# Later landings in the plan, one more known reader, and order lists searched anew, in a hybrid decoder block

## The chip, the cores and the metric

The kernel runs on one core of a Trainium2 chip. The metric is device time in microseconds from launch to end, the median of three runs. PE is the matrix engine (TensorE), DVE the vector engine, ACT the scalar engine, POOL the engine that issues the adding transfers (GpSimd), SP the engine that issues the loads (SyncE).

## What is computed

One decoder block over 256 positions of width 2048: a half-step SwiGLU feed-forward, a token mixer (a recurrent branch and a short gated convolution that share one input projection), and a second half-step feed-forward, with RMS norms between. The change touches the two feed-forwards alone:

```
def swiglu_ffn(x, w_gate, w_up, w_down):
    return (jax.nn.silu(x @ w_gate) * (x @ w_up)) @ w_down

x = x + 0.5 * swiglu_ffn(rms_norm(x, ffn1_norm), ffn1_w_gate, ffn1_w_up, ffn1_w_down)
...                                                   # the mixer
x = x + 0.5 * swiglu_ffn(rms_norm(x, ffn2_norm), ffn2_w_gate, ffn2_w_up, ffn2_w_down)
```

`w_gate` and `w_up` are 2048 by 5632, `w_down` 5632 by 2048, all float32.

## The kernel before

**Arithmetic.** A float32 operand is split into a high part (`hi`, a cast by ACT) and a low part (`lo`, the difference, by DVE). A product of two is three matmul passes: high by high and low by high (the "high products", `Unit.over`), and high by the weight's low part (the "low products", `Unit.under`). Each matmul takes a 128 by 128 block of the activations as the stationary operand and streams 512 columns of weights.

**Strips.** The 5632 columns of gate and up are eleven blocks of 512. One goes through plain products at the opening; the other ten go in pairs. A pair of blocks is a *strip*, and `sevens` (from L690 on) computes it by a two-by-two block scheme with seven products instead of eight: p0 to p6 for most of the depth, and plain products x01, x00, x11, x10 for the rows left over. Strip names give the matrix (g, u, d), the feed-forward (1 or 2) and a number: g1_4 is a gate strip of feed-forward 1, u1_4 its up strip, d1_2 a stage of down strips. The weights of p4, p5, p6 and p3 are sums of loaded blocks (w11, w12, w21, w22). DVE adds them in place in w11 (for p4, then for p5); some are added by a transfer that POOL issues (`by_transfer`, L719).

**Banks.** Sums gather in PSUM banks a, c, d and e. p0 goes to a, and ACT copies it to d ("seed"). p4 goes to bank c, and ACT takes a copy of it ("s5") before x01 adds to c; x01 starts bank e afresh. In a *joint* strip p4 goes to bank e, ACT copies e to c, and x01 adds onto both, so that one DVE addition of s5 at the end falls away. p5 and p6 leave the copies u2 and u3.

**Hidden units.** A gated result (`u_g`, `z`) of 128 by 512 is turned by eight transposes on PE for two positions' blocks (tile `ph`), and ACT and DVE then write its high and low parts into `h`, the stationary operand of the down strips. The items T, U are these turns in an order list. Tiles `split_..._x..` (the x weights of gate and up, under pair names "xa" and "xb") and `h` share one pool, `bigs`, of nine places: a new `h` takes a place that such a `split` tile may still hold, and its writers then wait until the last matmul has read it.

**What sets the order.** A table gives PE's order for each strip: `FINE_ORDERS` for gate and up (L31), `DOWN_ORDERS` for down (L65). The first letter says whether p3's sum is made by DVE (+, J) or by a transfer (-, j), J and j mean joint; 5 or 6 in gate and up says how the spare row is treated. For ACT, DVE, SP and POOL the class `Plan` (from L160) makes the order when the kernel is built: each step has an engine, a length, needs and a due time; `Plan.run` (L249) simulates the engines and takes the most pressing ready step. These orders are then fixed in the program. On the chip each engine runs its queue strictly in order, with semaphores for the needs; a step that waits holds all behind it. A load is planned with

```
step = self.add("SP", 0.45, fn, tail=1.5 + 0.71 * rows)
step.room, step.share = room, ("load", 1.35, 0.71 * rows, 0.6)
```

where 1.35 is the start and 0.6 the tail behind a queue that loads share with the adding transfers. The places `short`, one alone in gate and up, hold the x weights: the next x load is issued when DVE has read the one before.

`turn_item` (L1452) plans a turn and its two copies; `turn_cells` (L1529) calls it for T and U. The last turn of an up stage is handed over, with its PE step's end as the earliest time, to the next `down_stage` (L1621), which plans its copies. Neither knew of the `bigs` place that an `h` takes.

## Time and profile before

| | |
|---|---|
| median of three runs | 1711.32 us (1710.82 to 1712.18) |
| profiled execution, its own time | 1713.96 us |
| its span, first to last instruction | 1712.2 us |
| granted clock of PE, mean | 0.996 |
| matmuls on PE | 7706 |

| stage | span from the start, us | PE busy, us | granted clock |
|---|---|---|---|
| gate and up 1, first pairs (g1_1 to u1_2) | 200.4 to 363.5 | 162.65 of 163.10 | 1.00 |
| down d1_2 | 363.5 to 453.4 | 85.02 of 89.90 | 0.98 |
| g1_3 to u1_4 | 453.4 to 619.6 | 164.29 of 166.20 | 0.99 |
| down d1_4 | 619.6 to 704.0 | 84.40 of 84.40 | 1.00 |
| mixer | 704.0 to 1015.0 | 310.34 of 311.00 | 1.00 |
| g2_1 to u2_2 | 1205.7 to 1369.8 | 162.44 of 164.10 | 1.00 |
| down d2_2 | 1369.8 to 1453.5 | 83.08 of 83.70 | 1.00 |
| g2_3 to u2_4 | 1453.5 to 1619.9 | 164.39 of 166.40 | 0.99 |

How rows are read: in the order in time, a row is start, duration, engine, line, instruction, operands, shape, count, and in square brackets the engine's idle time before it with what ended it. Buffer numbers are left out, so `hi_g_p<-raw_g_w` may be any p's high part of a gate strip. L102 is the helper that records every instruction. In a row of stretches, PE, PEld, DVE, ACT and POOL busy time stand with their counts, then the granted clock, the share of the DMA engines and GB/s. The matmul's own duration includes its pipeline; rows of a run of matmuls are best compared from start to start.

### The profile page before, as it was taken

How to read it: one execution, taken by the hardware profiler on the slowest of the kernel's cores; microseconds unless marked ns; L12 is line 12 of the kernel's file. 1: busy time of each engine (PE TensorE's matmuls, PEld its weight loads, DVE VectorE, ACT ScalarE, POOL GpSimd, SP SyncE). 2: the span in 40 equal slices, each digit the busy share in tenths (PEclk: the TensorE clock that was granted, in tenths of full speed). 3: DMA queues.
4: the chain of work that ended last, by engine and by line, in shares of the span. 5: the costliest groups of instructions: out<-in, count | busy, mean ns of one | idle time of the engine just before them, and what ended most of it. 6: DMA issues, size and time to landing. Idle time of an engine off the chain costs nothing.

```text
span 1712.2 us, 20073 instructions
## 1 busy us (share of the span) xinstructions
PE 1688.8 (99%) x7706; PEld 1399.1 (82%) x7706; DVE 1557.0 (91%) x1281; ACT 1127.1 (66%) x1305; POOL 85.5 (5%) x107
## 2 busy tenths in 40 slices
PE   9999999989999999999999999999999999999997
PEld 7888888878887888888888888888887888887886
DVE  7989999989989998899997978998999899989996
ACT  6766576746675767688776665756666666756665
POOL 0200000000000000000000000000000000000000
PEclk9999999999999999999999999999999999999999
DMA  8786988867988868577856685967978777988784
GB/s 320 238 236 202 277 251 256 268 194 222 283 275 230 268 203 267 189 226 243 260 198 204 214 270 172 288 234 221 307 240 257 238 240 248 274 257 238 251 256 143
DMA packets 187744, 413.48 MB, mean 241 GB/s; under 512 B 8324, under 2 KB 11264, under 8 KB 184320
## 3 DMA queue, kind: packets, MB, share of 16 engines
q1 hardware_dynamic: 174912, 340.81, 56.2%
q0 software_dynamic: 12560, 70.33, 21.5%
q8 instruction: 60, 0.98, 0.2%
q10 hardware_dynamic: 176, 1.06, 0.2%
q14 instruction: 36, 0.29, 0.1%
HBM read 339.82 MB, written 2.10 MB: 200 GB/s over the span
## 4 chain that ended last, share of the span: by engine, by line
PE 89%; DVE 5%; DMA 2%; issue 2%; ACT 2%; DVEq 0%; SPq 0%; ACTq 0%
PE ps_g_a L102 10%; PE ps_d_a L102 9%; PE ps_u_a L102 8%; PE ps_d_c L102 6%; PE ps_g_c L102 6%; PE ps_u_c L102 5%; PE ps_d_d L102 4%; PE ps_u_d L102 3%; PE ps_d L102 3%; PE ps_d_e L102 3%; PE ps_g_d L102 3%; PE ps_in_b L102 3%; PE ps_in_x L102 3%; PE ps_u_e L102 3%; PE ps_o L102 3%; PE ps_u L102 2%
## 5 line engine op out<-in xcount | busy, mean ns | idle before, releaser
L102 DVE TENSOR_TENSOR lo_g_p<-raw_g_w,hi_g_p 128x3072 fp32r<-128x3072 f32 (+3 forms) x90 | 234.8, 2625 | 29.3 <-ACT hi_g_p L102 13.0
L102 ACT CAST hi_g_p<-raw_g_w 128x1536 fp32r<-128x1536 f32 (+1 forms) x140 | 200.1, 1466 | 79.0 <-DVE raw_g_w L102 25.0
L102 DVE TENSOR_TENSOR lo_u_p<-raw_u_w,hi_u_p 128x3072 fp32r<-128x3072 f32 (+3 forms) x90 | 221.2, 2464 | 21.6 <-ACT hi_u_p L102 21.5
L102 ACT CAST hi_u_p<-raw_u_w 128x1536 fp32r<-128x1536 f32 (+1 forms) x140 | 188.7, 1386 | 73.2 <-DVE raw_u_w L102 34.5
L102 ACT CAST hi_d_p<-raw_d_w 128x1024 fp32r<-128x1024 f32 x140 | 141.6, 1048 | 96.0 <-DVE raw_d_w L102 59.8
L102 DVE TENSOR_TENSOR lo_d_p<-raw_d_w,hi_d_p 128x2048 fp32r<-128x2048 f32 (+1 forms) x90 | 161.3, 1811 | 7.7 <-ACT hi_d_p L102 7.1
L102 DVE TENSOR_TENSOR raw_u_w<-raw_u_w,raw_u_w 128x1024 f32<-128x1024 f32 (+2 forms) x49 | 84.5, 1734 | 3.0 <-DMA raw_u_w<-in_ffn_w_up_dram 1.9
L102 ACT CAST hi_d_x<-raw_d_x 128x1024 fp32r<-128x1024 f32 x72 | 73.2, 1046 | 17.9 <-DMA raw_d_x<-in_ffn_w_down_dram 7.4
L102 DVE TENSOR_TENSOR lo_d_x<-raw_d_x,hi_d_x 128x2048 fp32r<-128x2048 f32 x36 | 82.0, 2285 | 2.6 <-ACT hi_d_x L102 2.1
L102 ACT CAST split_u_x<-raw_u_x 128x1024 fp32r<-128x1024 f32 x40 | 42.0, 1051 | 55.8 <-DMA raw_u_x<-in_ffn_w_up_dram 55.7
L102 PE MATMUL ps_u_a<-hi_u_p,xT_n 128*128 128x512 f32 x280 | 73.5, 390 | 0.0
L102 DVE TENSOR_TENSOR raw_g_w<-raw_g_w,raw_g_w 128x1536 f32<-128x1536 f32 (+2 forms) x41 | 70.8, 1752 | 0.3
L102 PE MATMUL ps_g_a<-hi_g_p,xT_n 128*128 128x512 f32 x280 | 70.3, 389 | 0.0
L102 ACT CAST split_g_x<-raw_g_x 128x1024 fp32r<-128x1024 f32 x40 | 41.9, 1047 | 40.9 <-DMA raw_g_x<-in_ffn_w_gate_dram 40.6
L102 PEld LDWEIGHTS ps_g_a<-hi_g_p,xT_n 128*128 128x128 f32 x280 | 52.6, 188 | 10.9
L102 PEld LDWEIGHTS ps_u_a<-hi_u_p,xT_n 128*128 128x128 f32 x280 | 52.3, 188 | 10.7
L717 POOL DMA_DIRECT2D raw_g_w<-raw_g_w x38 | 33.0, 867 | 553.7 <-DVE raw_g_w L102 333.9
L102 DVE TENSOR_TENSOR raw_d_w<-raw_d_w,raw_d_w 128x1024 f32<-128x1024 f32 (+1 forms) x43 | 54.6, 1293 | 0.3
L102 DVE TENSOR_TENSOR split_u_x<-raw_u_x,split_u_x 128x1024 fp32r<-128x1024 f32 x40 | 48.8, 1219 | 5.5 <-ACT split_u_x L102 5.5
L102 DVE TENSOR_TENSOR split_g_x<-raw_g_x,split_g_x 128x1024 fp32r<-128x1024 f32 x40 | 48.8, 1219 | 2.4 <-ACT split_g_x L102 2.4
L102 PE MATMUL ps_d<-hi_d,h 128*128 128x512 f32 x192 | 45.8, 391 | 0.0
L102 PEld LDWEIGHTS ps_d<-hi_d,h 128*128 128x128 f32 x192 | 35.8, 188 | 7.3
(579 smaller groups left out, 4178.3 us busy)
## 6 DMA issues: line engine op xcount, KB each, us to landing
raw_g_w<-in_ffn_w_gate_dram SPq DMA_DIRECT2D x40, 1024.0 KB, 6.7
raw_u_w<-in_ffn_w_up_dram SPq DMA_DIRECT2D x40, 1024.0 KB, 7.3
raw_d_w<-in_ffn_w_down_dram SPq DMA_DIRECT2D x40, 1024.0 KB, 6.8
raw_d_x<-in_ffn_w_down_dram SPq DMA_DIRECT2D x36, 1024.0 KB, 6.6
raw_g_w<-raw_g_w POOLq DMA_DIRECT2D x37, 768.0 KB, 8.2
raw_g_w<-in_ffn_w_gate_dram SPq DMA_DIRECT2D x40, 512.0 KB, 7.5
raw_g_x<-in_ffn_w_gate_dram SPq DMA_DIRECT2D x40, 512.0 KB, 5.6
raw_u_w<-in_ffn_w_up_dram SPq DMA_DIRECT2D x40, 512.0 KB, 7.7
```

The costliest lines, as they stand in the source:

```text
L102: ins = getattr(self.engine, name)(*args, **kwargs)
L717: nc.gpsimd.dma_start(raw[key]()[:, h, :], raw[other]()[:, h, :], accum_op=ALU.add)
```

## The change

Three things. A load and an adding transfer are planned to land 0.5 us later. The copies of a turned unit get one more need: the last low product of the `split` tile given up (`after`), and those handed over to the down stage start no earlier than the last such product of the stage (`used`). And the order lists are other ones: 14 of 20 for gate and up, 9 of 10 for down. Seven strips become joint and one ceases to be.

```
 def load(self, rows, fn, room):
-    step = self.add("SP", 0.45, fn, tail=1.5 + 0.71 * rows)
-    step.room, step.share = room, ("load", 1.35, 0.71 * rows, 0.6)
+    step = self.add("SP", 0.45, fn, tail=2.0 + 0.71 * rows)
+    step.room, step.share = room, ("load", 1.35, 0.71 * rows, 1.1)
...
-    z = plan.add("POOL", ..., tail=6.7 + 1.36 * more)
-    z.share = "sum", 1.8, 5.43 + 1.36 * more, 0.6
+    z = plan.add("POOL", ..., tail=7.2 + 1.36 * more)
+    z.share = "sum", 1.8, 5.43 + 1.36 * more, 1.1
...
-    return turned_parts(plan, high, low, a, at=since)
+    return turned_parts(plan, high, low, a, after, at=since)
...
-    turn_before = lambda z=before: turn_cells(plan, [z[1, 0], z[0, 0]], turned)
+    def turn_before(z=before, given_up=short_turn[1]):
+        turn_cells(plan, [z[1, 0], z[0, 0]], turned, after=plan.left[given_up].low)
...
-    return plan, tails, [(*z[:3], z[3].end - end) for z in later]
+    used = max(plan.left[p].low.end for p in ("xa", "xb") if p in plan.left)
+    return plan, tails, [(*z[:3], max(z[3].end, used) - end) for z in later]
...
 FINE_ORDERS, (2, 1), last list (u2_2); DOWN_ORDERS, (1, 2), first list
-["J5", "p0", "U", "p4", "p5", "x01", "p2", "x11", "p6", "x00", "p1", "T", "x10", "p3"]
+["J5", "p0", "p4", "x01", "p5", "p2", "x11", "p6", "x00", "U", "p1", "T", "p3", "x10"]
-["-", "p0", "T", "p4", "x01", "x11", "p5", "p1", "p6", "x00", "p3", "p2", "x10"]
+["j", "p0", "p4", "T", "x01", "x11", "p5", "p1", "p6", "x00", "p3", "p2", "x10"]
```

The program keeps every matmul, every transfer and every ACT instruction in number; DVE has 1275 instructions instead of 1281. Where they stand differs. Three places:

ACT at the entry of the down strip d1_2_0; `h1_6` is the unit turned last in the up strip. Before:

```order
L102 CAST split_u1_2_x10_2777<-raw_u1_2_x10_2754 128x1024
L102 CAST hi_d1_2_0_p0_2883<-raw_d1_2_0_w11_2875 128x1024
L102 CAST h1_6_2889<-ph1_6_1_2795 128x4x128
L102 CAST h1_6_2889<-ph1_6_0_2800 128x4x128
L102 CAST hi_d1_2_0_p0_2883<-raw_d1_2_0_w11_2875 128x1024
L102 CAST hi_d1_2_0_x01_2900<-raw_d1_2_0_x01_2879 128x1024
L102 CAST hi_d1_2_0_p4_2903<-raw_d1_2_0_w11_2875 128x1024
L102 CAST hs1_2_4_0_2906<-hv1_4_1_2891 128x512
L102 CAST hi_d1_2_0_x01_2900<-raw_d1_2_0_x01_2879 128x1024
L102 CAST hi_d1_2_0_p4_2903<-raw_d1_2_0_w11_2875 128x1024
```

With the change:

```order
L102 CAST split_u1_2_x10_2771<-raw_u1_2_x10_2737 128x1024
L102 CAST hi_d1_2_0_p0_2877<-raw_d1_2_0_w11_2873 128x1024 x2
L102 CAST hi_d1_2_0_x01_2893<-raw_d1_2_0_x01_2879 128x1024
L102 CAST hs1_2_4_0_2897<-hv1_4_1_2888 128x512
L102 CAST hi_d1_2_0_p4_2899<-raw_d1_2_0_w11_2873 128x1024
L102 CAST h1_6_2902<-ph1_6_1_2826 128x4x128
L102 CAST h1_6_2902<-ph1_6_0_2831 128x4x128
L102 CAST hi_d1_2_0_p4_2899<-raw_d1_2_0_w11_2873 128x1024
L102 CAST hi_d1_2_0_x01_2893<-raw_d1_2_0_x01_2879 128x1024
L102 CAST hi_d1_2_0_x11_2931<-raw_d1_2_0_x11_2881 128x1024 x2
```

The two copies of `h1_6` moved from between the two halves of p0 to behind p0, half of x01, `hs` and half of p4.

ACT at the start of the second gate strip g1_4, from the copy of p0 (seed) on. Before:

```order
L102 COPY ps_g1_4_d_4122<-ps_g1_4_a_4088 128x512
L102 CAST hi_g1_4_p5_4132<-raw_g1_4_w11_3904 128x1536
L102 ACTIVATE s5_g1_4_4148<-ps_g1_4_c_4115 128x512
L102 CAST hi_g1_4_p1_4150<-raw_g1_4_w21_4032 128x1536
L102 CAST hi_g1_4_p5_4132<-raw_g1_4_w11_3904 128x1536
L102 CAST hi_g1_4_p1_4150<-raw_g1_4_w21_4032 128x1536
```

With the change:

```order
L102 COPY ps_g1_4_d_4118<-ps_g1_4_a_4085 128x512
L102 CAST hi_g1_4_p1_4130<-raw_g1_4_w21_4031 128x1536
L102 ACTIVATE s5_g1_4_4144<-ps_g1_4_c_4111 128x512
L102 CAST hi_g1_4_p5_4146<-raw_g1_4_w11_3931 128x1536 x2
L102 CAST hi_g1_4_p1_4130<-raw_g1_4_w21_4031 128x1536
```

The copy s5 stood behind p5's first half; now p1's first half stands there and p5 comes after s5. In g2_2 and g2_4 the rows around s5 are the same in both programs; on DVE one of the two z's has moved there ahead of p4's first low part.

PE in the up strip u2_2, p4's low products and what follows. Before:

```order
L102 MATMUL ps_u2_2_e_10331<-lo_u2_2_p4_10292,xs2_0_8049 128x512 x4
L102 MATMUL ps_u2_2_e_10331<-lo_u2_2_p4_10292,xT_n2_0_7709 128x512
L102 MATMUL ps_u2_2_a_10287<-hi_u2_2_p5_10314,xs2_0_8049 128x512 x8
L102 MATMUL ps_u2_2_a_10287<-hi_u2_2_p5_10314,xT_n2_0_7709 128x512 x2
L102 MATMUL ps_u2_2_a_10287<-lo_u2_2_p5_10345,xs2_0_8049 128x512 x4
L102 MATMUL ps_u2_2_a_10287<-lo_u2_2_p5_10345,xT_n2_0_7709 128x512
L102 MATMUL ps_u2_2_e_10331<-split_u2_2_x01_10343,xT_n2_1_8088 128x512 x4
```

With the change:

```order
L102 MATMUL ps_u2_2_e_10307<-lo_u2_2_p4_10296,xs2_0_8041 128x512 x4
L102 MATMUL ps_u2_2_e_10307<-lo_u2_2_p4_10296,xT_n2_0_7701 128x512
L102 MATMUL ps_u2_2_e_10307<-split_u2_2_x01_10312,xT_n2_1_8079 128x512 x4
L102 MATMUL ps_u2_2_c_10333<-split_u2_2_x01_10312,xT_n2_1_8079 128x512 x4
L102 MATMUL ps_u2_2_e_10307<-split_u2_2_x01_10312,xT_n2_1_8079 128x512 x2
L102 MATMUL ps_u2_2_c_10333<-split_u2_2_x01_10312,xT_n2_1_8079 128x512 x2
L102 MATMUL ps_u2_2_a_10281<-hi_u2_2_p5_10321,xs2_0_8041 128x512 x8
```

x01 moved from behind p5 to directly behind p4, whose bank e it adds onto. In g2_3, which has become joint, x01 follows p4 directly before and after, but before it started bank e afresh, and now it adds onto p4.

## Prediction

> **What bounds the kernel now.** I read the page first, then the waits of PE, then the order in time around each wait.

> ```profile
> span 1712.2 us, 20073 instructions
> PE 1688.8 (99%) x7706; PEld 1399.1 (82%) x7706; DVE 1557.0 (91%) x1281; ACT 1127.1 (66%) x1305; POOL 85.5 (5%) x107
> ```

> PE sets the end, and the change leaves it every matmul: only the instructions' order differs. The most that can go is PE's 1712.2 - 1688.8 = 23.4 us of idle time and the time in which its matmuls run slowly. PE's waits:

> ```profile
> PE ps_g_c L102 <- ACT s_g L102: 5.5, 4, 1.8
> PE ph L102 <- DVE z L102: 3.2, 2, 2.6
> PE ps_d_a L102 <- ACT hi_d_p L102: 1.2, 1, 1.2
> PE ps_d_a L102 <- DVE lo_d_p L102: 1.1, 1, 1.1
> PE ps_u_a L102 <- DVE lo_u_p L102: 0.2, 1, 0.2
> ```

> The last row is that of the window 1060 to 1712; it shows what a small wait costs. The four large ones fall at five places, all in the feed-forward stages, and I price each from start to start of PE's rows, which takes in slow matmuls. Undisturbed, eight products take 1.81 us (619.61 to 621.42), 0.2266 each.

> **The first entry, down strip d1_2 (A).**

> ```profile
> 363.50 1.07 PE L102 MATMUL ps_d_a<-hi_d_p,h 128*128 128x512 f32 x4
> 363.70 1.07 ACT L102 CAST h<-ph 128x512 fp32r<-128x512 f32 x2 [7.56 <-PE ps_u_d L102]
> 371.84 1.45 PE L102 MATMUL ph<-ident,z 128*128 128x128 f32 x8 [2.55 <-DVE z L102]
> 372.95 3.55 PE L102 MATMUL ps_d_c<-hi_d_p,hs 128*128 128x512 f32 x8
> 376.34 1.09 PE L102 MATMUL ps_d_c<-lo_d_p,hs 128*128 128x512 f32 x4
> ```

> ACT stood 7.56 us before two copies of a turned unit `h`, until the last product of the up strip had read the tile whose place `h` takes. Behind them in ACT's queue were p0's second half, x01 and p4; so PE came to a standstill four matmuls into the strip. The plan did not know this wait. The change tells it, and its order has the copies behind p0, half of x01, hs and half of p4, and the turn T behind p4. That is the arrangement which d1_4 has already:

> ```profile
> 617.13 1.07 ACT L102 CAST h<-ph 128x512 fp32r<-128x512 f32 x2
> 619.61 1.98 PE L102 MATMUL ps_d_a<-hi_d_p,h 128*128 128x512 f32 x8
> 621.42 1.07 PE L102 MATMUL ps_d_a<-lo_d_p,h 128*128 128x512 f32 x4
> 624.14 1.07 PE L102 MATMUL ps_d_e<-lo_d_p,hs 128*128 128x512 f32 x4
> 625.06 1.03 PE L102 MATMUL ph<-ident,z 128*128 128x128 f32 x8
> 625.25 0.57 ACT L102 COPY ps_d_c<-ps_d_e 128x512 f32<-128x512 f32 x1 [1.10 <-PE ps_d_e L102]
> 625.88 2.12 PE L102 MATMUL ps_d_e<-hi_d_x,h 128*128 128x512 f32 x8
> ```

> There p0, p4 and T took 625.88 - 619.61 = 6.27 us without a wait. In d1_2 p0, T and eight of p4's twelve took 376.34 - 363.50 = 12.84; the same work at d1_4's rate is 6.27 - (625.06 - 624.14) = 5.35. **A = 7.49 gained.** In d1_2 the copies may start 0.2 us after the last up product, ahead of the d1_4 case, with 24 matmuls (5.4 us) before x01 needs them. Bounds: at worst the z's and low parts on DVE still hold PE as now, and 2.55 of the 7.49 stay; at best all goes. I take the upper end, since d1_4 is the same order on the same engines.

> **The second entry, d2_2 (B)** changes likewise:

> ```profile
> 1369.84 1.98 PE L102 MATMUL ps_d_a<-hi_d_p,h 128*128 128x512 f32 x8
> 1376.34 1.08 PE L102 MATMUL ps_d_c<-lo_d_p,hs 128*128 128x512 f32 x4
> ```

> 6.50 against 5.35: **B = 1.15.** There is one new thing: h2_3's copies now stand before p0's halves. They need the turn U, which in u2_2's list stands behind 123 products: from 1327.89 (its row stands below) that is 27.9 us, so U ends near 1357, and p0 starts at 1369.84. Those 12 us cover them; without that cover a late pair costs about the 1.07 that two copies took at 617.13.

> **The second gate strips (C, D, E).** After p4 ACT takes a copy `s5` of bank c, and PE's x01 waits for it.

> ```profile
> 542.64 1.08 PE L102 MATMUL ps_g_e<-split_g_x,xT_n 128*128 128x512 f32 x4
> 543.52 1.47 ACT L102 CAST hi_g_p<-raw_g_w 128x1536 fp32r<-128x1536 f32 x1 [4.21 <-DVE raw_g_w L102]
> 545.54 1.20 PE L102 MATMUL ps_g_c<-split_g_x,xT_n 128*128 128x512 f32 x4 [1.82 <-ACT s_g L102]
> 548.10 2.98 PE L102 MATMUL ps_g_a<-hi_g_p,xs 128*128 128x512 f32 x8
> 550.91 0.62 PE L102 MATMUL ps_g_a<-hi_g_p,xT_n 128*128 128x512 f32 x2
> 546.00:551.00 5.00, 5.00 (x17) 3.92 (x16) 4.65 (x4) 4.54 (x4) 1.49 (x2) 0.66 0.57 156
> 1298.00:1303.00 5.00, 5.00 (x24) 4.13 (x23) 4.64 (x4) 5.00 (x5) 1.63 (x2) 1.00 0.60 160
> ```

> In g1_4 the copy stands behind p5's first high half, which stood 4.21 us until DVE had summed its rows. From 542.64 to 550.91 are 20 products, 4.53 us at full rate: 8.27 - 4.53 = 3.74 lost, of which 1.8 is the wait and the rest slow matmuls: the granted clock behind it is 0.66. The new order puts p1's half, which needs no sum, before s5 and p5 behind it. **C = 3.74.** If p1's transfer were late instead, half of it would be back.

> In g2_2 and g2_4 p5's half still stands before s5:

> ```profile
> 1286.40 1.05 ACT L102 CAST split_g_x<-raw_g_x 128x1024 fp32r<-128x1024 f32 x1 [6.17 <-DMA raw_g_x<-in_ffn_w_gate_dram]
> 1288.86 1.76 DVE L102 TENSOR_TENSOR lo_g_p<-raw_g_w,hi_g_p 128x1536 fp32r<-128x1536 f32 x1 [1.67 <-ACT hi_g_p L102]
> 1291.20 0.74 DVE L102 SCALAR_TENSOR_TENSOR z<-ps_u_d,r_n,z 128x512 f32<-128x512 f32 x1
> 1294.66 1.07 PE L102 MATMUL ps_g_e<-split_g_x,xT_n 128*128 128x512 f32 x4
> 1299.33 0.84 PE L102 MATMUL ps_g_a<-hi_g_p,xs 128*128 128x512 f32 x3
> 1542.94 1.07 PE L102 MATMUL ps_g_e<-split_g_x,xT_n 128*128 128x512 f32 x4
> 1551.23 0.62 PE L102 MATMUL ps_g_a<-hi_g_p,xT_n 128*128 128x512 f32 x2
> ```

> x01's transfer landed late, ACT's casts of p4 came after it, and DVE idled 1.67 us before p4's low part, then ran two z's (this one 0.74, the other alike) between its halves. The new order has one z ahead of the first half, in that idle time: s5 comes 0.74 earlier. g2_2 loses 4.67 - 2.72 (12 products) = 1.95 now and 1.21 then: **E = 0.74.** g2_4 loses 8.29 - 4.53 = 3.76 now; its up strip's tail takes the form that u2_1 had before g2_2 (T, p3, then the last x), so I give it g2_2's 1.21, short enough for the clock to hold as at 1298: **D = 2.55.** Bounds for both: nothing gained, or all 5.71.

> **What the change adds.** g1_2 ran without a wait worth naming; u1_1 before it now ends as u2_1 did, so it gets g2_2's lag: **F = -1.21** (bounds 0 and -3.76).

> Six more DVE additions go than come (seven strips turn joint, one turns back), which no path sees directly. But joint means that x01 adds onto p4's bank, so it must wait until ACT has copied that bank. In the d1_4 rows this took from 625.06 to 625.88, 0.82 us after p4's last issue, and T's transposes filled it. In u2_2 and g2_3 x01 now follows p4 at once, and ACT has a half of p2 ahead of the copy:

> ```profile
> 1327.89 2.43 PE L102 MATMUL ps_u_a<-hi_u_p,xT_n 128*128 128x512 f32 x10
> 1336.80 0.59 ACT L102 COPY ps_u_c<-ps_u_e 128x512 f32<-128x512 f32 x1
> 1460.47 1.48 ACT L102 CAST hi_g_p<-raw_g_w 128x1536 fp32r<-128x1536 f32 x1 [1.10 <-PE ps_g_c L102]
> 1461.63 1.07 PE L102 MATMUL ps_g_e<-split_g_x,xT_n 128*128 128x512 f32 x4
> ```

> g2_3: p2's half from 1460.47 to 1461.95, copy 0.59, 0.06 to PE: 1462.60 against 1461.63, 0.97. u2_2: p0 from 1327.89, p4's high products end 25 x 0.2266 later (1333.56), p2's half 0.2 behind, then copy: 1335.89 against 1334.69, 1.20. **G = -2.17** (0.82 each at least, 0.82 + 1.48 each at most, -1.64 to -4.60).

> 23 of the 30 lists are new, each with other neighbours; I allow a third of them one small wait of 0.2: **H = -1.4** (0 to -3.5). Transfers cost nothing themselves: none is added, and SP issues the same 420.

> **Sum.** 7.49 + 1.15 + 3.74 + 2.55 + 0.74 = 15.67; less 1.21, 2.17 and 1.4: 10.89. The profiled execution took 1713.96, 2.64 above the median; I take the gain from the median: 1711.32 - 10.89 = **1700.4**.

> [...]

> **Rivals.**
> 1. *The half microsecond suffices*: x01 is no longer late, so s5 is on time in g1_2, g2_2 and g2_4. Then D and E are 5.71 and F is 0: 10.89 + 2.42 + 1.21 = 14.5, 1696.8. For it: only the landing separates g2_2 from a strip without loss. Against: SP still issues x01 at the same place behind the same weights.
> 2. *The waits move rather than go*: C, D, E and F at their old prices elsewhere (D, E nothing gained, F -3.76, C half) and H -3.5. 7.49 + 1.15 + 1.87 - 3.76 - 2.17 - 3.5 = 1.1, 1710.2; half-way to the forecast it is 6.0, 1705.3. For it: ten strips carry the p5-before-s5 risk whenever DVE lags. Against: the plan now expects later landings.
> 3. *Slower: joint copies late*. If ACT is one cast (1.48) late at p4's end, the two bare places cost 2.30 and, above 1.8, the slow clock (3.74 - 1.82 = 1.92) too, 8.4 together; d1_2, d2_2, d2_4 and u1_4, where transposes cover only the 0.82, cost 1.48 each, 5.9; with F at 3.76 and H 1.4 that is 19.5 against 15.67: 3.8 slower, 1715.1. It decides from one whole cast of lag. Against: at d1_4 ACT was waiting 1.10 for PE.
> 4. *The slow clock is not the waits'*: it stays where they go. C and D lose 1.92 each, A 3.55 - 1.98 = 1.57: 10.89 - 5.41 = 5.5, 1705.8. For it speaks that behind the 1.66 in g2_2 the clock held; against it, where 0.66 stood. [...]
> That the plan does not do as told is excluded: the new order shows the copies moved.

> **How the numbers follow.** Forecast 0.56, rival 1 0.12, rival 2 0.20, rival 3 0.08, rival 4 0.04. The range 1695.0 to 1708.5 holds rivals 1 and 4, and half of 2. 0.2% is 3.4 us, about what can be told from no change: faster means below 1707.9. The forecast and rivals 1 and 4 (0.72) give that, and 0.12 of rival 2; the rest of it and 0.03 of rival 3 are the same; 0.05 is slower. Faster 0.84, same 0.11, slower 0.05.

> **What would show it.** A and B: d1_2 and d2_2 run from p0 to x01 in some 6.3 us, and ACT's 7.56 before `h` is gone. C: no PE wait on s_g near 540, granted clock 1.00 there. D, E, F: PE waits of about 1.2 on s_g in g2_2, g2_4 and g1_2. G: two waits of about 1 us on ps_g_c and ps_u_c copies. Wrong would be PE idle time above 18 us, a granted clock under 0.8 in any of these strips, or new waits of PE on lo_d_p.

## The result, and the profile after

The changed kernel took 1698.41 us (median of four runs, 1697.13 to 1701.71) against 1711.61 us before: a ratio of 0.9926, 95% interval 0.9909 to 0.9943. The forecast was 1700.4. A second group of runs gave 1698.88 us and 0.9905 (0.9888 to 0.9921) beside a kernel before that took 1716.15 there; since the kernel before differs by 4.5 us between groups of runs, later runs are compared by their ratios to the kernel before of their own group.

First the page of the profiled execution (its own time 1701.71), then PE's waits in it, longest first (total, count, longest):

```profile
span 1699.9 us, 20055 instructions
PE 1683.5 (99%) x7706; PEld 1398.4 (82%) x7706; DVE 1553.7 (91%) x1275; ACT 1128.4 (66%) x1305; POOL 85.7 (5%) x107
```

```profile
PE ps_g_a L102 <- ACT u_g L102: 3.3, 1, 3.3
PE ps_u_e L102 <- ACT ps_u_c L102: 0.9, 1, 0.9
PE ps_g_e L102 <- ACT ps_g_c L102: 0.7, 1, 0.7
PE ps_in_x_d L102 <- ACT ps_in_x_d L102: 0.7, 1, 0.7
PE ps_u_a L102 <- DVE lo_u_p L102: 0.2, 1, 0.2
```

All four large waits of before are gone: no `s_g`, no `ph <- z`, no `hi_d_p` or `lo_d_p`. Two small ones (0.9 and 0.7, the second and third row) are the copies of the joint strips; the 0.7 on `ps_in_x_d` is in the mixer and was there before. One large wait is new, on `u_g`.

The entry of d1_2, in order of time, shows A. From p0 to x01 it takes 369.38 - 363.00 = 6.38 us, and ACT's copies of `h` wait for nothing:

```profile
362.91 1.07 ACT L102 CAST h<-ph 128x512 fp32r<-128x512 f32 x2
363.00 2.09 PE L102 MATMUL ps_d_a<-hi_d_p,h 128*128 128x512 f32 x8
369.38 2.12 PE L102 MATMUL ps_d_e<-hi_d_x,h 128*128 128x512 f32 x8
```

The stretches of the strips g1_4, g2_2, g2_3 and g2_4 (length, busy time of PE, PEld, DVE, ACT and POOL with counts, granted clock, DMA share, GB/s):

```profile
526.14:565.79 39.65, 39.65 (x178) 32.68 (x176) 35.68 (x24) 25.99 (x25) 1.76 (x3) 1.00 0.88 248
1274.11:1313.64 39.53, 39.53 (x176) 32.59 (x174) 35.63 (x22) 25.77 (x24) 2.64 (x4) 1.00 0.89 245
1439.37:1485.03 45.66, 41.65 (x175) 33.67 (x174) 37.33 (x24) 27.62 (x25) 5.11 (x6) 0.96 0.87 255
1526.05:1565.57 39.52, 39.52 (x176) 32.58 (x175) 37.86 (x24) 25.06 (x23) 2.59 (x3) 1.00 0.90 253
```

A gate strip without a wait takes 39.5 us. Before, g1_4, g2_2 and g2_4 took 43.20, 41.39 and 43.22 (start to start of the strips). All three are now without loss. g2_3, which took 39.61, is 6.05 longer. Why is seen in its rows in order of time: SP's issue of the transfer of x11, two adding transfers issued by POOL, ACT's cast of x11, the copy `u_g`, and PE's first products of p6:

```profile
1445.90 0.37 SPq L102 DMA_DIRECT2D raw_g_x<-in_ffn_w_gate_dram  x1
1449.57 0.86 POOL L717 DMA_DIRECT2D raw_g_w<-raw_g_w  x1 [7.28 <-DVE lo_g_p L102]
1452.43 0.86 POOL L717 DMA_DIRECT2D raw_g_w<-raw_g_w  x1 [2.00 <-DVE lo_g_p L102]
1458.54 1.05 ACT L102 CAST split_g_x<-raw_g_x 128x1024 fp32r<-128x1024 f32 x1 [7.38 <-DMA raw_g_x<-in_ffn_w_gate_dram]
1462.24 0.59 ACT L102 ACTIVATE u_g<-ps_g_a 128x512 f32<-128x512 f32 x1
1462.88 3.56 PE L102 MATMUL ps_g_a<-hi_g_p,xs 128*128 128x512 f32 x8 [3.27 <-ACT u_g L102]
1462.50:1467.50 5.00, 4.62 (x13) 3.70 (x14) 5.00 (x2) 3.06 (x3) 0.00 (x0) 0.66 1.02 386
```

The x11 transfer was issued at 1445.90 and ACT could cast it only at 1458.54, 12.6 us later. Behind that cast stand the casts of p1 and then `u_g`, without which PE may not overwrite bank a. PE waited 3.27 us and then ran at a granted clock of 0.66 (last row). The strip loses 6.05, of which 0.89 is the joint copy: 5.16 for this wait.

By stages, before minus after in the two profiled executions:

| place | predicted | measured |
|---|---|---|
| A, d1_2 | 7.49 | 7.24 |
| B, d2_2 | 1.15 | 1.05 |
| C, g1_4 | 3.74 | 3.55 |
| D, g2_4 | 2.55 | 3.70 |
| E, g2_2 | 0.74 | 1.86 |
| F, g1_2 | -1.21 | 0.15 |
| G, copies in u2_2 and g2_3 | -1.20, -0.97 | -1.20, -0.89 |
| H, all else | -1.4 | -5.16 in g2_3, +2.0 elsewhere |
| sum | 10.89 | 12.3 |

The 12.3 is the difference of the spans, 1712.2 - 1699.9, and the +2.0 is what the other rows leave of it. The measured rows A to F are differences in the length of the stage, from start to start of PE's rows; so is G for u2_2, and g2_3's 6.05 is shared out as said above.

### The profile page after: what moved, and what is told of

The parts are those of the page before. It is cut to its first block, busy times and chain, and to the rows that moved or that the text cites. A ratio compares the mean times of both kernels' runs of the same rounds, so it can differ in the third digit from the quotient of the medians.

```text
span 1699.9 us, 20055 instructions
## 1 busy us (share of the span) xinstructions
PE 1683.5 (99%) x7706; PEld 1398.4 (82%) x7706; DVE 1553.7 (91%) x1275; ACT 1128.4 (66%) x1305; POOL 85.7 (5%) x107
## 4 chain that ended last, share of the span: by engine, by line
PE 97%; DMA 1%; ACT 1%; DVE 0%; issue 0%; DVEq 0%; ACTq 0%
PE ps_g_a L102 11%; PE ps_u_a L102 10%; PE ps_d_a L102 9%; PE ps_g_c L102 6%; PE ps_u_c L102 5%; PE ps_d_c L102 5%; PE ps_u_d L102 4%; PE ps_d_d L102 4%; PE ps_g_d L102 4%; PE ps_d_e L102 4%; PE ps_d L102 4%; PE ps_u_e L102 4%; PE ps_in_b L102 3%; PE ps_in_x L102 3%; PE ps_o L102 3%; PE ps_u L102 2%
## 5 line engine op out<-in xcount | busy, mean ns | idle before, releaser
L102 DVE TENSOR_TENSOR lo_g_p<-raw_g_w,hi_g_p 128x3072 fp32r<-128x3072 f32 (+3 forms) x90 | 234.6, 2625 | 25.4 <-ACT hi_g_p L102 11.8
L102 ACT CAST hi_g_p<-raw_g_w 128x1536 fp32r<-128x1536 f32 (+1 forms) x140 | 200.7, 1467 | 79.6 <-DVE raw_g_w L102 32.6
L102 ACT CAST hi_u_p<-raw_u_w 128x1536 fp32r<-128x1536 f32 (+1 forms) x140 | 189.5, 1385 | 79.8 <-PE ps_u_c L102 29.8
L102 DVE TENSOR_TENSOR lo_u_p<-raw_u_w,hi_u_p 128x3072 fp32r<-128x3072 f32 (+3 forms) x90 | 221.2, 2465 | 18.6 <-ACT hi_u_p L102 18.3
L102 ACT CAST hi_d_p<-raw_d_w 128x1024 fp32r<-128x1024 f32 x140 | 140.5, 1047 | 90.4 <-DVE raw_d_w L102 50.4
L102 DVE TENSOR_TENSOR lo_d_p<-raw_d_w,hi_d_p 128x2048 fp32r<-128x2048 f32 (+1 forms) x90 | 161.6, 1812 | 6.5 <-ACT hi_d_p L102 5.9
L102 ACT CAST hi_d_x<-raw_d_x 128x1024 fp32r<-128x1024 f32 x72 | 73.1, 1050 | 26.7 <-DMA raw_d_x<-in_ffn_w_down_dram 14.6
L102 DVE TENSOR_TENSOR lo_d_x<-raw_d_x,hi_d_x 128x2048 fp32r<-128x2048 f32 x36 | 82.1, 2285 | 5.8 <-ACT hi_d_x L102 5.8
L102 DVE TENSOR_TENSOR raw_u_w<-raw_u_w,raw_u_w 128x1024 f32<-128x1024 f32 (+2 forms) x49 | 84.6, 1734 | 1.0 <-DMA raw_u_w<-in_ffn_w_up_dram 0.2
L102 PE MATMUL ps_u_a<-hi_u_p,xT_n 128*128 128x512 f32 x280 | 73.8, 391 | 0.0
L102 DVE TENSOR_TENSOR raw_g_w<-raw_g_w,raw_g_w 128x1536 f32<-128x1536 f32 (+2 forms) x41 | 71.0, 1753 | 0.3
L102 PE MATMUL ps_g_a<-hi_g_p,xT_n 128*128 128x512 f32 x280 | 70.6, 390 | 0.0
L102 ACT CAST split_g_x<-raw_g_x 128x1024 fp32r<-128x1024 f32 x40 | 41.9, 1048 | 33.8 <-DMA raw_g_x<-in_ffn_w_gate_dram 33.7
L102 PEld LDWEIGHTS ps_g_a<-hi_g_p,xT_n 128*128 128x128 f32 x280 | 52.8, 189 | 11.0
L102 PEld LDWEIGHTS ps_u_a<-hi_u_p,xT_n 128*128 128x128 f32 x280 | 52.2, 188 | 10.6
L102 DVE TENSOR_TENSOR split_g_x<-raw_g_x,split_g_x 128x1024 fp32r<-128x1024 f32 x40 | 48.8, 1219 | 9.0 <-ACT split_g_x L102 9.0
L102 ACT CAST split_u_x<-raw_u_x 128x1024 fp32r<-128x1024 f32 x40 | 42.0, 1049 | 20.3 <-DMA raw_u_x<-in_ffn_w_up_dram 20.1
L102 DVE TENSOR_TENSOR raw_d_w<-raw_d_w,raw_d_w 128x1024 f32<-128x1024 f32 (+1 forms) x43 | 54.7, 1294 | 0.3
L102 DVE TENSOR_TENSOR split_u_x<-raw_u_x,split_u_x 128x1024 fp32r<-128x1024 f32 x40 | 48.8, 1220 | 5.0 <-ACT split_u_x L102 5.0
L102 PE MATMUL ps_d<-hi_d,h 128*128 128x512 f32 x192 | 45.8, 391 | 0.0
L102 PE MATMUL ps_g_a<-hi_g_p,xs 128*128 128x512 f32 x160 | 41.2, 402 | 3.3 <-ACT u_g L102 3.3
```

The source lines that it names most:

```text
L102: ins = getattr(self.engine, name)(*args, **kwargs)
```

## Experiment 1: the three parts of the change, apart

The theory T: the planner's two edits carry the gain. Its rival L: the new lists do. Four kernels: the planner alone, the need alone, the change without the need, and the change without the later landing.

Planner alone (both tables as before):

```
-FINE_ORDERS, DOWN_ORDERS: the changed lists
+FINE_ORDERS, DOWN_ORDERS: the lists of before
```

> The changed planner (landing 0.5 us later and the need of the h copies) with the order lists of before. Theory T, the planner's two edits carry most of it: the entries d1_2 and d2_2 run without a wait (7.2 and 1.05 gained, as in the changed kernel), g1_4 has x01's cast instead of p5's before s5 (3.55 gained), g2_4 likewise (3.7), g2_2 keeps p5 before s5 (0 to 1.9): 1711.6 - 15.5 = 1696, and without the two bare joint copies. Rival L, the new lists carry what happens at s5 in g2_2 and g2_4 because they free the x weights' place earlier: waits on s5 of 1.7 to 1.8 us stay in both, 1711.6 - 11.8 = 1699.8.

Measured 1724.03 us, ratio 1.0051 (1.0038 to 1.0063): slower than before, which neither theory had (1696 and 1699.8 expected). PE's waits in its profile, the three largest groups, and one of the rows behind them:

```profile
PE ps_u_a L102 <- ACT hi_u_p L102: 5.0, 4, 1.6
PE ps_g_d L102 <- DVE lo_g_p L102: 3.5, 2, 1.7
PE ps_g_d L102 <- ACT hi_g_p L102: 3.2, 2, 1.6
549.09 3.05 PE L102 MATMUL ps_g_d<-hi_g_p,xT_n 128*128 128x512 f32 x12 [1.58 <-ACT hi_g_p L102]
```

No wait on s5 above 0.4 us is left, as wished: in g1_4 and g2_4 x01 is now cast 4.76 us after the strip's start, behind the copy of p0, where it was cast 0.1 after the start before. But p1's and other halves now come late: the waits moved on to the products behind (the last row is p1 in g1_4), and g1_3, u2_2 and g2_4 were each 3.0 to 3.5 us longer than with the need alone (next kernel). This is what the prediction's rival 2 describes, in a kernel that the prediction did not look at.

The need alone:

```
-step = self.add("SP", 0.45, fn, tail=2.0 + 0.71 * rows)
+step = self.add("SP", 0.45, fn, tail=1.5 + 0.71 * rows)
...   # the adding transfers and the queue's tails likewise; both tables as before
```

> Only the need of the h copies, landing and lists as before. Theory T: d1_2 runs from p0 to x01 in 6.3 us (7.2 gained), d2_2 in 6.3 (1.05), and g1_4 has p1's half in place of p5's before s5 (3.55); g2_2 and g2_4 keep their waits of 1.7 and 1.8: 1711.6 - 11.8 = 1699.8. Rival: the need alone only moves the wait (another step stands behind h or DVE's z's hold PE for 2.55 at d1_2): 1711.6 - 7.2 + 2.55 = 1707.

Measured 1707.29 us, ratio 0.9958 (0.9945 to 0.9972). d1_2 is 82.52 us long against 89.93, so the need by itself brings 7.41 there: it is enough for A. B is only 0.41 of the 1.05, and C is not the need's at all. In g1_4 p1's half joined p5's in front of s5 instead of taking its place, and PE waited longer than before:

```profile
PE ps_g_c L102 <- ACT s_g L102: 6.8, 5, 3.1
528.88 1.05 ACT L102 CAST split_g_x<-raw_g_x 128x1024 fp32r<-128x1024 f32 x1 [4.79 <-DMA raw_g_x<-in_ffn_w_gate_dram]
540.86 1.21 PE L102 MATMUL ps_g_c<-split_g_x,xT_n 128*128 128x512 f32 x4 [3.05 <-ACT s_g L102]
540.80:544.80 4.00, 3.94 (x17) 3.25 (x18) 3.64 (x3) 3.70 (x4) 1.34 (x2) 1.00 0.58 153
```

Here x01 was still late, cast 0.30 us after the strip's start. (The last row, the granted clock behind the wait, is used in experiment 5.)

The change without the need:

```
-return turned_parts(plan, high, low, a, after, at=since)
+return turned_parts(plan, high, low, a, at=since)
...
-return plan, tails, [(*z[:3], max(z[3].end, used) - end) for z in later]
+return plan, tails, [(*z[:3], z[3].end - end) for z in later]
```

> The changed kernel without the need of the h copies (landing and lists as changed). The copies of h stand again between the halves of p0 at d2_2 and d2_4, as at d1_2 before. Theory T, the need carries the gain at the entries: ACT waits up to 7 us for the last up products at both, PE loses some 7.2 at each, 1698.4 + 14 = 1712; less where the place given up is read earlier. Rival L, the joint down lists with T behind p4 carry it and cover the late copies: no more than 1.5 at each, 1698.4 to 1701.

Measured 1708.97 us, ratio 0.9962 (0.9949 to 0.9974). The loss that d1_2 had before is back, in d2_2:

```profile
1357.25 1.07 ACT L102 CAST h<-ph 128x512 fp32r<-128x512 f32 x2 [7.60 <-PE ps_u_d L102]
1359.32 0.96 PE L102 MATMUL ps_d_a<-hi_d_p,h 128*128 128x512 f32 x3 [1.25 <-ACT hi_d_p L102]
1362.02 1.20 PE L102 MATMUL ps_d_a<-lo_d_p,h 128*128 128x512 f32 x4 [1.50 <-DVE lo_d_p L102]
1365.48 0.50 PE L102 MATMUL ps_d_e<-hi_d_p,hs 128*128 128x512 f32 x1 [2.27 <-ACT hi_d_p L102]
```

The stage was 8.5 us longer than in the changed kernel (91.1 against 82.6). d2_4, whose copies stood in the same place, lost nothing, so the theory's price holds at one place of two. The joint lists with T behind p4 do not cover a late `h`.

At d1_2 itself, though, nothing came back: the stage is 82.69 us long without the need, as in the changed kernel, and ACT's copies of `h` stand where they stand there, behind half of p4:

```profile
362.89 1.07 ACT L102 CAST h<-ph 128x512 fp32r<-128x512 f32 x2
```

So A has two sufficient causes: the need with the old lists, or the new lists and the later landing without it. What the need adds to the new lists is that the loss does not turn up at another entry. The new lists alone, without need and landing, were not run.

The change without the later landing:

```
-step = self.add("SP", 0.45, fn, tail=2.0 + 0.71 * rows)
+step = self.add("SP", 0.45, fn, tail=1.5 + 0.71 * rows)
...   # the adding transfers and the queue's tails likewise; both tables as changed
```

> The changed kernel with the landing of before (need and lists as changed). Both z's stand again between the halves of p4's low part in g1_2, g2_2 and g2_4, and p5's half before s5 in g1_2 and g2_4. Rival L, the lists free x01's place earlier so it is cast before the strip begins: no wait on s5 above 0.3, 1698.4 within 1.5. Theory T, the half microsecond carries it: waits on s5 of 1.2 to 1.8 in g1_2 and g2_4, 2.4 to 7.4 together with slow matmuls, 1701 to 1706.

Measured 1702.04 us, ratio 0.9924 (0.9912 to 0.9937): within its interval the changed kernel. Small waits on s5 came back,

```profile
PE ps_g_c L102 <- ACT s_g L102: 3.3, 6, 1.3
```

six of them, 3.3 us, the longest 1.3, none followed by slow matmuls: 1.3 us leave PE 2.1 of a window of 3.41 us, and the clock fell only behind 1.59 or less (experiment 5). But x01 was early in g1_4 and g2_4 all the same: cast 1.48 and 2.57 us before the strips began, as in the changed kernel (1.48 and 2.63), where the need alone had 0.30 and 0.31 after. So the big losses there were the lists' to remove. In these ratios the half microsecond is worth something between nothing and 0.2% with the new lists. With the old lists it costs 1.0051 - 0.9958 = 0.93%, some 16 us. Neither theory was right as a whole: need and lists together carry the gain, and the landing can only be judged with the lists searched for it.

## Experiment 2: four lists

If the lists make x01 early, the lists of the up strips ahead should be enough, since x01 is loaded when DVE has read the up strip's last x. The edit to the kernel with the need alone puts the changed kernel's lists in for u1_1, u1_3, u2_1 and u2_3; the first of them:

```
 (1, 1), second list (u1_1)
-["+5", "p0", "p4", "p5", "x01", "p2", "x11", "p6", "p1", "x10", "T", "x00", "p3"],
+["J5", "p0", "p4", "p5", "x01", "p2", "x11", "p6", "p1", "x00", "T", "p3", "x10"],
```

> The kernel with the need alone (landing and lists as before), but the four lists of the up strips ahead of g1_2, g1_4, g2_2 and g2_4 (u1_1, u1_3, u2_1, u2_3) are the changed ones. Theory U: these lists take the last x of the up strip earlier from its place, so the next x01 is loaded and cast earlier: x01's cast 1.1 to 2.6 us before the strips g1_4 and g2_4 begin (0.3 after them with the need alone), waits on s5 below 0.7 in g1_4, g2_2 and g2_4 instead of 3.05, 1.39 and 1.82, 1.2 to 2 + 2.6 + 0.9 + 2 = some 6 us faster than the need alone (ratio 0.992 to before). Rival: the gain at s5 comes from the whole set of lists or from the landing; x01's cast stays at 0.0 to 0.3 after the strips' beginning and the ratio stays at 0.996.

Measured 1700.53 us, ratio 0.9918 (0.9904 to 0.9932), against 0.9958 for the need alone and 0.9926 and 0.9905 for the whole change. DVE's reading of the last x of u2_3 and SP's issue of g2_4's x01, first in the kernel before, then in this one:

```profile
1527.47 1.22 DVE L102 TENSOR_TENSOR split_u_x<-raw_u_x,split_u_x 128x1024 fp32r<-128x1024 f32 x1
1528.71 0.37 SPq L102 DMA_DIRECT2D raw_g_x<-in_ffn_w_gate_dram  x1
```

```profile
1515.52 1.22 DVE L102 TENSOR_TENSOR split_u_x<-raw_u_x,split_u_x 128x1024 fp32r<-128x1024 f32 x1
1516.77 0.37 SPq L102 DMA_DIRECT2D raw_g_x<-in_ffn_w_gate_dram  x1
PE ps_g_c L102 <- ACT s_g L102: 2.1, 5, 0.8
```

SP issues within 0.03 us of the end of the reading in both. Before, that was 6.07 us ahead of the strip's start (1534.78); now it is 8.43 ahead (1525.20). x01 was then cast 2.39 us before the start, and g2_4's wait on s5 is gone. In g1_4 it fell from 3.05 to 0.46 and in g2_2 from 1.39 to 0.28. The waits on s5 together fell from 6.8 to 2.1 (last row). So four lists, all of them of strips *ahead* of the losses, carry most of C, D and E without the later landing: g1_4, g2_2 and g2_4 gain 7.9 us against before, where the changed kernel gains 9.1 and the need alone 2.0.

In all three SP issues x01 earlier than with the need alone, by 2.3 to 3.3 us against the strip's start. That this earlier load is what does it fits the rows, but was not isolated: the lists move other steps too. In g1_2 theory U does not hold: its x01 is issued later (8.46 us ahead of the start against 11.45), and the strip is 0.4 longer than before.

## Experiment 3: the new wait in g2_3

Is the 3.27 us wait a property of the order or of the execution? The changed kernel a second time, one with x11's cast held back, and one with g2_3's old list:

> The changed kernel once more, for a second profile. Theory W, the wait of 3.27 us in g2_3 comes from a race of x11's transfer with the adding transfers and falls in some executions only: here either a u_g wait of 0 to 1 (span some 1695 on the first chip's scale, g2_3 40.5 us long), or again above 3 (45.7); the scatter of the times is some 4 us. Rival: it is a fixed property of the order (x11's cast before u_g): the wait is again 3.0 to 3.5 and g2_3 45.7 us long.

Measured 1698.88 us (1697.72 to 1700.34), and this time no wait on `u_g`; g2_3 was 40.48 us long. x11's cast and the copy behind it:

```profile
1454.97 1.05 ACT L102 CAST split_g_x<-raw_g_x 128x1024 fp32r<-128x1024 f32 x1 [2.64 <-DMA raw_g_x<-in_ffn_w_gate_dram]
1458.68 0.59 ACT L102 ACTIVATE u_g<-ps_g_a 128x512 f32<-128x512 f32 x1
```

The transfer was again issued 6.53 us after the strip's start, but was cast 7.9 us later instead of 12.6. What differed ahead of it: the strip's first two adding transfers were issued 1.25 before and 0.35 after its start here, against 0.89 and 2.06 after in the first profile. That they held up x11 was not isolated, and other traces speak against so simple a rule: without the need the two were issued 0.06 before and 1.04 after the start, and x11 landed after 7.9 us; with its cast held (next edit) they came 0.86 before and 1.15 after, and it landed after 9.8. What delays the transfer stays open.

The edit that holds the cast:

```
 made[key] = Unit(plan, f"{name}_{key}", rows_x, pair, raw[key], [loads[key]], [loads[key]], one)
+if name == "g2_3" and key == "x11":
+    made[key].hi[0].needs.append(made["u2"])
```

> The changed kernel with x11's cast in g2_3 held in ACT's order behind the copy u_g. Theory W: no wait on u_g whatever x11's landing, g2_3 40.5 us long (0.89 for the joint copy), scatter below that of the changed kernel, median 1 to 2 below it. Rival: the lateness moves on: PE waits for x11 itself or for p1 in the same strip, 1 to 3 us, and the median is the changed kernel's.

Measured 1697.33 us (1697.24 to 1698.3), ratio 0.9894 (0.988 to 0.9909). No wait on `u_g`, g2_3 40.57 us long, and four runs within 1.1 us, where the changed kernel's eight span 4.6. The median is 1.5 below the changed kernel's of the same group, but the intervals overlap. The rival holds in part: the next strip, u2_3, is 41.51 us long against 41.01 in the changed kernel's second profile, so holding the cast costs 0.5 there.

The old list for g2_3:

```
-["j6", "p0", "p4", "x01", "p5", "p2", "p6", "x11", "p1", "x10", "p3", "x00"],
+["-6", "p0", "p4", "x01", "p5", "p2", "p6", "x11", "p1", "x10", "p3", "x00"],
```

> The changed kernel with the list of before for g2_3 (not joint; p4 to c, the copy s5). Prediction's step G: the bare joint copy goes, 0.89 gained, and x11's cast stands behind u_g as well, so that wait goes too: g2_3 39.6 us long, 0.9 faster than the kernel with x11 held, 2 to 3 faster than the changed one. Rival: s5 is late instead (p5 before s5, as it was in g2_2 before): a wait of 1.2 or more there, no gain.

Measured 1697.71 us, ratio 0.9895 (0.988 to 0.991). g2_3 was 39.85 us long, 0.7 less than with x11 held, so the joint copy's price is real. But the next strip, u2_3, met a wait that the others do not have and took 42.25 us, 0.74 more than with x11 held, so nothing was gained in sum:

```profile
PE ps_u_a L102 <- ACT hi_u_p L102: 0.9, 1, 0.9
```

## Experiment 4: the copy in u2_2, and both repairs

```
 (2, 1), last list (u2_2)
-["J5", "p0", "p4", "x01", "p5", "p2", "x11", "p6", "x00", "U", "p1", "T", "p3", "x10"],
+["J5", "p0", "p4", "U", "x01", "p5", "p2", "x11", "p6", "x00", "p1", "T", "p3", "x10"],
```

> The changed kernel with U moved directly behind p4 in u2_2 and behind x00 no longer, the form u2_4 has. Prediction's step G: the transposes cover the joint copy as at d1_4, the wait of 0.92 before x01 goes and u2_2 is 1.0 us shorter; d2_2 unchanged. Rival: U's transposes wait for their own inputs there, or the casts of h behind U hold up ACT ahead of the copy: 0.5 to 2 us lost in place of the 1.08.

Measured 1696.84 us, ratio 0.9892 (0.9878 to 0.9907). u2_2 was 42.26 us long against 43.17 in the changed kernel of the same group, and the wait of 0.92 is gone: eight transposes cover the copy, and the strip is only 0.31 longer than before (41.95). g2_3's wait was there again in this profile, smaller than the first time; x11 landed after 10.3 us, between the 7.9 and the 12.6 of the two others, in the same order of instructions:

```profile
PE ps_g_a L102 <- ACT u_g L102: 1.0, 1, 1.0
```

Both repairs together:

> The changed kernel with both repairs: x11's cast in g2_3 held behind u_g, and U directly behind p4 in u2_2. If the two are independent: 0.9 to 1.0 off the 1697.3 of the first alone, 1696.4, with a scatter of about 1, some 1.1% below the kernel before. Rival: U's earlier copies of h take ACT's time ahead of d2_2 and the gain is given back there: 1697.3.

Measured 1696.7 us (1696.36 to 1697.4), ratio 0.9898 (0.9885 to 0.9912), span 1694.7. Stage by stage both gains are there (u2_2 42.27; g2_3 40.80 without the wait). In time it cannot be told from the changed kernel: the intervals overlap. What is better is that its four runs lie within 1.1 us.

## Experiment 5: which waits cost the clock

The prediction took the slow matmuls behind a wait as part of its price. A wait of 3.05 us in the kernel with the need alone was followed by a granted clock of 1.00 (its row stands in experiment 1). So waits of graded length were set into the changed kernel:

```
-act.activation(snaps[key], to(n)(), AF.Copy, scale=scales[key]() if scales else scale)
+for _ in range(EXTRA.get(name, 0) + 1 if key == "s5" else 1):
+    act.activation(snaps[key], to(n)(), AF.Copy, scale=scales[key]() if scales else scale)
```

> The changed kernel; before x01's second half can start, ACT repeats the copy s5 in nine strips, 2 to 8 times more, so that PE waits there some 0.5 us for each: about 1.0 (g1_1), 1.5 (g1_2), 2.0 (u1_2), 2.5 (g1_3), 1.5 (g1_4), 2.0 (g2_1), 2.5 (u2_1), 3.0 (g2_2), 3.9 (g2_4). Rule of length: every wait above 1.7 us is followed by slow matmuls (granted clock below 0.9 in the 4 us behind it), none below. Rule of phase: waits of 1.5 to 3 are followed by them or not, whatever their length, by where they fall. [...]

> The same program once more. Rule of length: the same waits are followed by a slow clock as in the first look. Rule of phase: at least one wait between 1.5 and 3.0 us changes sides, since the place of the wait against a free-running window differs from execution to execution.

Measured 1727.2 and 1725.11 us, one execution each. The wait in g1_3 with the granted clock of the 4 us around its end, in the first execution and then in the second (L103 is the recording helper, one line lower here):

```profile
463.62 2.07 PE L103 MATMUL ps_g_c<-split_g_x,xT_n 128*128 128x512 f32 x4 [2.95 <-ACT s_g L103]
465.50 1.05 PE L103 MATMUL ps_g_e<-split_g_x,xT_n 128*128 128x512 f32 x2
463.00:467.00 4.00, 3.38 (x9) 2.69 (x10) 2.03 (x2) 4.00 (x4) 0.00 (x0) 0.57 1.00 201
```

```profile
463.08 1.20 PE L103 MATMUL ps_g_c<-split_g_x,xT_n 128*128 128x512 f32 x4 [2.94 <-ACT s_g L103]
464.11 0.62 PE L103 MATMUL ps_g_e<-split_g_x,xT_n 128*128 128x512 f32 x2
463.00:467.00 4.00, 3.92 (x17) 3.25 (x18) 2.58 (x2) 3.71 (x4) 0.33 (x1) 1.00 0.89 179
```

The same wait of 2.95 us in the same program is followed by four matmuls in 1.88 us (465.50 - 463.62) in one execution and in 1.03 (464.11 - 463.08) in the other. Length alone does not decide: the rule of length falls. Over both executions, the eight waits of 1.65 to 1.70 all kept the clock (1.00 in the 4 us from 293 and in those from 334, in either execution), both of 2.32 lost it (0.70 and 0.61 in the 4 us from 1216), and so did those of 3.56 and 3.74 (0.79 and 0.57 in the 4 us from 1304) and of 4.8. Outside the scan, the 1.82 in g1_4 before lost it (0.66 in the prediction's row) and a 1.82 in g2_4 with the need alone kept it (1.00), as the 3.05 did.

Where the wait falls decides, and the traces show against what. While matmuls run, the granted clock falls to 0.50 for 3.413 us at a time, and within one execution all falls begin on a grid of that step: in the kernel before at 372.70, 546.78 and 1546.88, which lie 51 and 293 steps apart ((546.78 - 372.70) / 51 = 3.413, (1546.88 - 546.78) / 293 = 3.413). On this grid one can see how much of a wait lies in one window. First the 1.82 of g1_4 before, then the 3.05 with the need alone, then the 2.95 of the scan in its first and in its second execution (length, PE's busy time, and third from the end the granted clock):

```profile
543.37:546.78 3.41, 1.59 (x7) 1.05 (x6) 3.41 (x4) 3.26 (x4) 0.00 (x0) 1.00 0.75 168
546.78:550.19 3.41, 3.41 (x9) 2.64 (x8) 3.06 (x3) 3.41 (x4) 0.86 (x1) 0.50 0.41 122
```

```profile
536.20:539.61 3.41, 1.61 (x8) 0.99 (x6) 3.41 (x3) 2.15 (x2) 0.00 (x0) 1.00 0.91 182
539.61:543.02 3.41, 2.16 (x9) 1.79 (x10) 3.05 (x3) 3.41 (x4) 0.82 (x1) 1.00 0.48 157
```

```profile
459.85:463.26 3.41, 0.82 (x4) 0.36 (x2) 2.76 (x3) 3.25 (x7) 0.86 (x1) 1.00 0.76 225
463.26:466.67 3.41, 3.05 (x7) 2.47 (x8) 1.70 (x2) 3.41 (x4) 0.00 (x0) 0.50 1.07 213
```

```profile
457.95:461.37 3.42, 2.19 (x10) 1.49 (x8) 3.42 (x3) 3.32 (x5) 0.14 (x1) 1.00 0.99 254
461.37:464.78 3.41, 1.70 (x7) 1.42 (x8) 1.06 (x3) 3.35 (x5) 0.72 (x1) 1.00 0.84 186
```

The 1.82 lies whole in one window, which leaves PE 1.59 us busy, and the clock falls at its end. The 3.05 is split over two windows, with 1.61 and 2.16 busy, and the clock holds. The scan's two executions differ in the same way: 0.82 busy in one window, 2.19 and 1.70 in two. The same wait begins 0.82 us behind a point of the grid in the first (463.62 - 2.95 - 459.85) and 2.19 in the second (463.08 - 2.94 - 457.95): the grid is each execution's own. In all fourteen traces, from 30 us to the last matmul, twelve windows have PE busy for 1.59 us or less, and these twelve are followed by a fall. The others, some 6800, have 1.61 or more, and none is. So the rule of phase holds, and it has a bound: in these traces a window with PE busy for less than about 1.6 of its 3.41 us costs the clock of the next one. The bound was read off these traces afterwards, and PE's busy time has modelled ends, so it is no exact figure.

No wait had to fill a window of 3.41 us for a fall here: the 1.82 of g1_4 before and the two of 2.32 in the scan were enough.

## Why the prediction was right, and where it was not

The time lay 2.0 us below the forecast, inside the range, and the forecast's place, 0.9936 as a ratio, lies in the first group's interval. It does not lie in the second group's (0.9888 to 0.9921), whose 0.9905 is the range's lower end. That the sum came so close was in part luck: in the profiled execution D, E and F brought 3.6 us more than forecast and H 1.8 less. In the second profile, where the wait in g2_3 did not come, the spans differ by 1712.2 - 1696.0 = 16.2 us instead of the 10.89.

- **A and B right.** 7.49 and 1.15 forecast, 7.24 and 1.05 measured; taking d1_4 as the pattern was sound. For A the need alone is enough (7.41), and so are the new lists and the landing without it. B is the need's only to 0.41; the rest is the lists'.
- **C right in size, wrong in cause.** The prediction saw p1's half take p5's place ahead of s5. That move needs the lists and the landing together. Most of the loss goes with p5 left where it was, once x01 is early (experiment 2: 2.87 of the 3.55, with 0.46 of wait left), so the move can be worth 0.7 at most. The step that failed is "the new order puts p1's half, which needs no sum, before s5": true of the order, not what carries most of the gain.
- **D, E and F wrong, by 3.6 us together.** The forecast gave g2_4 and g1_2 "g2_2's lag", read from the form of the up strip's tail. Measured was no lag in any of the three. What the prediction had left out is when DVE reads the up strip's last x. The new lists bring this 2.4 us earlier in u2_3 and 2.1 in u1_3, counted to the next strip's start, and SP issues x01 as much earlier. The prediction had named x01's late transfer and DVE's idle 1.67 behind it, but it priced only the move of one z, 0.74, and held against rival 1 that SP issues x01 "at the same place". E and F are not explained by this: x01 of g2_2 was issued only 0.5 earlier and that of g1_2 1.9 later than before, yet they were cast 1.4 and 0.7 earlier. Why these landed sooner stays open.
- **G right**: 1.20 and 0.97 forecast, 1.20 and 0.89 measured, and covering the copy with transposes brings 0.9 back, as d1_4 had suggested.
- **H wrong in kind.** No spread of small waits came: elsewhere 2.0 us were gained. One large wait came instead, 5.16 us with its slow matmuls in the profiled execution, none in the second profile, and 1.5 in that of the kernel with u2_2 covered. Behind it stood one of the prediction's own signs of being wrong, a granted clock under 0.8 (0.66), in a strip where it had looked for the copy alone. The risk was visible in the order: x11's cast stands ahead of `u_g` in g2_3, where it stood behind it before.
- **Rivals.** Rival 1 named the right outcome at s5, 14.5 and 1696.8, and for the most part the wrong cause: without the half microsecond x01 is just as early in g1_4 and g2_4, and what the landing takes away are the small waits on s5 (3.3 us). As a ratio rival 1 is 0.9915; the first group's 0.9926 lies between it and the forecast, the second's 0.9905 below both. Rival 2 is what the planner alone does, 8.4 us slower than before. Rival 3, joint copies late by a cast, did not occur: 0.92 and 0.74 were the waits. Rival 4 is refuted as a statement on this change (C and D gained their slow matmuls), yet its doubt was justified: whether a wait costs the clock depends on where it falls (experiment 5).

The gain is uncertain by one thing that stays open in part: the kernel before took 1711.6 in one group of runs and 1714.7 to 1716.2 in the three others (on chips 13, 7 and 9), the changed one 1698.4 and 1698.9. Two of its waits, 1.82 and 1.83, leave PE 1.59 and 1.58 us busy in their windows, right at the bound of experiment 5, so a small shift can decide whether they cost the clock. In the 25 executions of the three groups a lower clock does go with a longer time: the three with a granted clock of 0.994 took 1716.3 on average, the five with 0.997 or 0.998 took 1713.4. Whether this or the chip sets the first group apart is not shown.

## What to carry to other kernels

When a plan fixes the order on engines that run strictly in order, a need that it doesn't know holds up everything queued behind it: ACT stood 7.56 us before two copies that take 1.07 together, and PE lost 7.4. Telling the plan of the reader brought that back; other orders can avoid the place by chance and meet the loss elsewhere, as d2_2 did. Lists searched for one set of planner rules say nothing about another: the same half microsecond cost 0.9% under the old lists and nothing that could be measured under the new ones, so a rule and a search are to be timed together. A transfer that lands late can be mended upstream, where the place it fills is given back (with four lists of the strips ahead, the wait on s5 in g1_4 fell from 3.05 us to 0.46), and a cast that waits for a transfer should not stand ahead of a copy that frees a bank; here moving it back narrowed the spread, while a gain in time could not be told.
